# Low parts of the weights by an accumulating DMA instead of a subtraction, in a two-block fp32 transformer on one core

## The chip, the cores and the metric

The program runs on 1 core of a Trainium2 chip. The metric is device time in microseconds (us) of one execution; the kernel before takes 2588.35 us (median of 3 runs, 2588.29 to 2590.03).

Engines are named as the profile names them: PE (TensorE, matrix products), PEld (its weight loads), DVE (VectorE), ACT (ScalarE), POOL (GpSimd), SP (SyncE, which here only issues DMAs). A DMA that SP issues goes to the queue q1 (hardware_dynamic in the profile), one that POOL issues to q0 (software_dynamic). "L138" is line 138 of the kernel before.

## What is computed

512 tokens of width 1024 pass through two transformer blocks in float32. The first has a mixer (convolution branch and attention side by side), attention to a memory of 256 tokens, and a gated feed-forward with a short convolution. The second has two layers of feed-forward, mixer, feed-forward; its mixers are a pooling one and latent attention. Every part follows a normalisation and is added to the residual:

```python
h = rmsnorm(x, norm_mix_pre[l])
y = parallel_mixer(h, w_in[l], conv_dw[l], ..., w_out[l], tabs)
x = x + rmsnorm(y, norm_mix_post[l])
y = memory_cross_attention(rmsnorm(x, norm_mem_pre[l]), mem_n, w_mem_q[l], w_mem_kv[l], w_mem_o[l])
x = x + rmsnorm(y, norm_mem_post[l])
y = conv_gated_ffn(rmsnorm(x, norm_ffn_pre[l]), w_up[l], ffn_dw[l], ffn_dw_b[l], w_down[l])
x = x + rmsnorm(y, norm_ffn_post[l])
...
def swiglu(h, w_gate, w_up, w_down):
    return (jax.nn.silu(h @ w_gate) * (h @ w_up)) @ w_down
x = x + FFN_HALF * swiglu(h, ffn1_w_gate[i], ffn1_w_up[i], ffn1_w_down[i])
x = x + pool_mixer(h, pool_w[j], pool_scale[j])        # or mla_mixer(h, ...)
x = x + FFN_HALF * swiglu(rmsnorm_2(x, ffn2_norm[i]), ffn2_w_gate[i], ...)
```

Nearly all the work is in products of the 512 tokens with weights, some 225 MB of them in float32.

## The kernel before

**Products in three passes.** PE multiplies in the type float32r, which keeps fewer bits than float32. Each weight and each activation is therefore held as two parts: `hi`, the value rounded to float32r, and `lo`, what is left of it. `mm3` (L165) issues three matmuls for a product: `hi` by `hi` (L168), `hi` by the activation's `lo` (L169), and the weight's `lo` by `hi` (L170).

**Weight units.** A unit is 128 partitions of 1024 columns (512 KB; 44 or so are of 768 columns), eight 128 x 128 tiles. `load_unit` (L149) makes one: `fetch` (L127) has SP bring it into a `raw` buffer; `cook` (L132) has ACT round it into `whi` (L138), and then DVE or POOL subtract, `wlo = raw - whi` (L140). `linear` (L172) goes over output tiles, and for each over the units and their eight tiles, 24 matmuls of 512 columns per unit. There are 428 units from `load_unit`; one more, the first of all (`raw0`, L91), is cooked in four pieces. `raw`, `whi` and `wlo` have 3 buffers each, so a unit's parts can be made as soon as PE has finished with the unit three before.

**Who subtracts.** `lo_on_pool` (L144) gives a share of the units, in fourths, to POOL; the rest go to DVE. The share is set by stage: all units in the input products and the attention of the first mixer (`W_IN`, `W_KV` = 4, from L660), none for the output product, a fourth in the memory stage, none from the convolutional feed-forward on (L827).

**The other work.** In the first mixer DVE runs 24 convolution taps for each of four channel tiles (L556), six more taps run on PE with diagonal matrices that POOL builds (`dg`, L530); POOL also makes stacked parts of the queries (`st`, L426), rotary sums (`m`, L416), low parts of memory tiles (L187) and scales softmax rows (`p`, L402). In a `swiglu` stage (L867) DVE takes PSUM out (`g`, L877), ACT applies silu (L879), POOL multiplies gate by value (L882), ACT and DVE make the parts of the result (`ah` L185, `al` L187), which the second product of the stage reads. Between the stages of the first block `settle` (L349) and `pre` (L321) bring the normed result into the residual and make the new activations' parts (`xh`, `xl`, L189 and L190), with a Newton iteration on DVE (`newton`, L223) that starts from `q` (L217).

**The order of the work.** Within an engine instructions run in the order that a scheduler of the language gives them, from a simulated timeline; an instruction that waits for a semaphore holds everything behind it on its engine, or in its engine's DMA queue.

Of the kernel before, what the change touches and what calls it, by code (L numbers as in the profile page):

```python
# [26 lines left out]
# order of the taps' offsets: the even ones from the middle, then the odd ones  # L27
# [33 lines left out]
class Kern:  # L61
# [3 lines left out]
    def __init__(self, ctx, tc, a, out):  # L65
# [6 lines left out]
        self.wr = E(tc.tile_pool(name="wr", bufs=3))  # L72
        self.wh = E(tc.tile_pool(name="wh", bufs=3))
        self.wl = E(tc.tile_pool(name="wl", bufs=3))
# [3 lines left out]
        self.sp = E(tc.tile_pool(name="sp", bufs=8))  # L78
        self.yp = E(tc.tile_pool(name="yp", bufs=16))
        self.yq = E(tc.tile_pool(name="yq", bufs=3))  # L80
        self.pps = {n: E(tc.tile_pool(name=n + "_psum", bufs=b, space=bass.MemoryType.PSUM))
                    for n, b in (("ps", 2), ("sc", 2), ("pt", 2), ("po", 1), ("mi", 1))}
        self.wturn, self.wshare = 0, 0
# [19 lines left out]
    # -- small access helpers --  # L103
# [17 lines left out]
    def turn(self, out, src):  # L121
        """Transpose by PE, which moves float32 words unchanged."""
        n = src.shape[0]
        return self.nc.tensor.transpose(out, src, self.ident[:n, :n])  # L124

    # -- weights: DRAM -> raw -> exact parts hi + lo --
# [5 lines left out]
    def cook(self, raw, n, pieces=1):  # L132
        hi = self.wh.tile([P, UNIT], F32R, name="whi", tag="whi")
        lo = self.wl.tile([P, UNIT], F32R, name="wlo", tag="wlo")
        w = n // pieces
        for i in range(pieces):
            s = slice(i * w, (i + 1) * w)
            self.nc.scalar.copy(hi[:, s], raw[:, s])  # L138
            eng = self.nc.gpsimd if self.lo_on_pool() else self.nc.vector
            eng.tensor_tensor(out=lo[:, s], in0=raw[:, s], in1=hi[:, s].bitcast(F32),  # L140
                              op=ALU.subtract)
        return hi, lo

    def lo_on_pool(self):  # L144
        """Share of the units (in fourths) whose low part GpSimd makes."""
        self.wturn = (self.wturn + 1) % 4
        return self.wturn < self.wshare

    def load_unit(self, src, n=UNIT):  # L149
        return self.cook(self.fetch(src, n), n)  # L150
# [6 lines left out]
    def load_tile(self, w, nt, nk):  # L157
        """Stationary tiles of output tile nt: list over k of (hi, lo) [P, P]."""
        res = []
        for k0 in range(0, nk, 8):  # L160
            n = min(8, nk - k0)
            res += self.tiles(self.load_unit(w[nt, :, k0 * P:(k0 + n) * P], n * P), n)
        return res

    def mm3(self, ps, w, x, start, stop):  # L165
        """ps += w.T @ x with w, x each given as exact (hi, lo) parts."""
        mm = self.nc.tensor.matmul
        mm(ps, w[0], x[0], start=start, stop=False)  # L168
        mm(ps, w[0], x[1], start=False, stop=False)  # L169
        self.mmi = mm(ps, w[1], x[0], start=False, stop=stop)  # L170
# [10 lines left out]
    # -- split an fp32 tile (SBUF or PSUM), optionally scaled per partition --  # L181
# [17 lines left out]
    # -- reciprocal square roots --  # L199
    # Sums over partitions land as [32 * j + r, t]: row r of token block j; transposed, they and  # L200
    # what is made of them stand in columns, [t, j, r].
    def sums(self, pairs, nb=4, ps=None, o=0, start=True, stop=True):
        """pairs: list of (selector [P, 32], squares [P, nb * P])."""
# [9 lines left out]
    def columns(self, sm, dim, eps=0.0, w=1):  # L213
        """sm / dim + eps in columns [P, block, w], in PSUM."""
# [8 lines left out]
    def newton(self, v, n):  # L223
        """rsqrt of v [P, n] on the vector engine."""
# [14 lines left out]
    def rstd(self, sqs, dim, nb=4):  # L239
        """rsqrt(mean + eps) in columns from squares [P, nb * P], summed over the list."""  # L240
        sm = self.sums([(self.c("ones"), sq) for sq in sqs], nb)
        v = self.columns(sm, dim, EPS)
        return self.newton(v.rearrange("p j r -> p (j r)"), nb)

    @staticmethod
    def per_block(R, w):
        """The columns of the four token blocks, each repeated w times."""
        return R.unsqueeze(2).to_broadcast([P, 4, w])

    def inner_rstd(self, sm, dim, R, w=1, post=1.0):  # L250
        """post * R * rsqrt(R^2 * sm / dim + eps): the norm of rows that still lack the factor R."""
# [16 lines left out]
    def bcast_ps(self, R, nb=4, w=1):  # L268
        """Columns to rows of all partitions (row r of w in its share of them), exact float32."""
# [14 lines left out]
    def expand(self, R, w, tag="t"):  # L284
        """Columns -> [32 * block + r, tokens], zero outside the block, as exact parts."""
# [13 lines left out]
    def spread(self, X, r, tag="mi"):  # L299
        """Row r of every block, on all partitions."""  # L300
# [6 lines left out]
    # -- residual stream --  # L307
# [5 lines left out]
    def gather(self, sqs, sq, last, w=S):  # L313
        """Sum of squares so far: at most two tiles, the last one kept apart."""
# [6 lines left out]
    def pre(self, gname, dve_squares=(), tag2="xs"):  # L321
        """Gain times x as exact parts, and the reciprocal rms in quadrant form."""
# [14 lines left out]
    def post_collect(self, gname, tag="xs"):  # L337
        """Evacuation of a stage's output that a norm follows; pre() of the next stage adds it."""
# [10 lines left out]
    def settle(self):  # L349
        """Generator: adds the pending normed output to x, a tile a step."""  # L350
# [40 lines left out]
    # ------------------------------------------------------------------  # L391
    def softmax_rows(self, ps, w, f, tag):
        """softmax over ps[:, :w] * f (f: [P, 1], positive)."""
# [12 lines left out]
    def rope(self, src, g, gs, cos, sin):  # L406
        """Rotary embedding along the partitions (pairs 16 apart), gains g, gs folded in."""
# [11 lines left out]
    def stack(self, src, r, tag, on_pool=False):  # L419
        """Exact parts of the 64 rows src[64 r:], one in each half of a tile."""  # L420
# [8 lines left out]
    # -- block 1: parallel mixer --  # L429
    def mem_load(self, i):  # L430
        """Two 256-token tiles of the memory side by side."""
# [16 lines left out]
    def mem_prep(self):  # L448
        """Gain times memory as exact parts."""
# [14 lines left out]
    def mem_kv(self):  # L464
        """Generator: key and value projections of the memory, a weight unit a step."""
# [49 lines left out]
    W_IN, W_KV, W_OUT, W_MEM = 4, 4, 0, 1  # L515

    def tap(self, n):
        """Output and input ranges of tap n."""
        d = TAPS[n]
        return (slice(0, S - d), slice(d, S)) if d >= 0 else (slice(-d, S), slice(0, S + d))  # L520

    def conv_pe(self, i, at):
        """The taps of channel tile i that run on PE, as products with diagonal matrices."""
# [18 lines left out]
    def conv_taps(self, i, at, acc):  # L542
        """Generator: the other taps of channel tile i, on DVE."""
# [17 lines left out]
    def mixer(self):  # L561
# [15 lines left out]
        # n-tiles: 0..7 (gate_i, val_i), 8 k, 9 v, 10..13 q pairs  # L577
# [31 lines left out]
        def ev_k(nt, ps):  # L609
# [6 lines left out]
            # both halves of a tile hold the same kv head  # L616
# [9 lines left out]
        def ev_v(nt, ps):  # L626
# [5 lines left out]
            # [s, 64 of kv0 | 64 of kv1] per token tile; zero-padded copies per kv head  # L632
# [25 lines left out]
        for n, nt in enumerate(self.ORDER):  # L658
            if n == 2:
                self.wshare = self.W_IN  # L660
# [9 lines left out]
        self.wshare = self.W_KV  # L670
# [4 lines left out]
        # attention, one head ahead  # L675
# [46 lines left out]
        self.wshare = self.W_OUT  # L722
        # attention's part of the product first
# [13 lines left out]
    def conv_norm(self, accs, cv):  # L737
        """Generator: layernorm over the conv channels, then silu, as exact parts."""
# [17 lines left out]
        for i in range(4):  # L756
# [6 lines left out]
            # silu(n) = 0.5 * n * (1 + tanh(n / 2))  # L763
# [10 lines left out]
    # -- block 1: cross attention to the memory --  # L774
    def memory(self):
        nc = self.nc
        a = self.a
        self.wshare = self.W_MEM
# [48 lines left out]
        self.wshare = 0  # L827

    # -- block 1: conv-gated ffn --
# [36 lines left out]
    # -- block 2: swiglu --  # L866
# [28 lines left out]
    # -- block 2: pooling mixer --  # L895
    # The linear map and the pooling commute: z = rstd * (W^T (g x)) in token-major form,
    # then the window sum minus count times the token as a product with a banded matrix
    # of integers, over the count.
    def pool_mixer(self):
# [30 lines left out]
        for u, zs in enumerate(zu):  # L930
            for gg in range(2):
                g = 2 * u + gg
                B = bands[g]
                # B[0]: [first block | next | 0 | 0]; B[1]: [0 | block | next | 0]
                for n in range(2):
# [12 lines left out]
                    # the first tokens have shorter windows  # L948
# [7 lines left out]
    # -- block 2: rope tables from the positions --  # L956
# [40 lines left out]
    # -- block 2: latent attention --  # L997
# [6 lines left out]
    def mla(self):  # L1004
# [32 lines left out]
        # keys  # L1037
# [19 lines left out]
        # values: [tokens, 4 heads x 128] per chunk  # L1057
# [14 lines left out]
        # queries: per pair of heads, two nope tiles and one tile of both rope parts  # L1072
# [92 lines left out]
    def key_rstd(self, ksum, pesum, Rkv):  # L1165
        """rsqrt of the mean square of a head's key: the nope part still lacks Rkv."""
# [46 lines left out]
def _stat(w):  # L1213
    """[K, N] -> [N / 128, 128, K]: stationary tiles, each partition's data contiguous."""
# [46 lines left out]
def _axial_rope():  # L1261
    """Cosines and signed sines of the grid positions, [2, 128, tokens]."""
# [21 lines left out]
def host_arrays(i):  # L1284
# [35 lines left out]
    # w_in: (gate_i, val_i) pairs, k, v, q head pairs (i, 4 + i)  # L1320
# [9 lines left out]
    # [att | conv, u, p, (2 n-tiles, 4 k, 128)]  # L1330
# [9 lines left out]
    # [c, u, p, (kk, 512)]  # L1340
# [15 lines left out]
    # [u, p, (gg, kk, 256)]  # L1356
# [12 lines left out]
    # keys [u, p, (hh, k, 128)]; values [c, p, (k, 4 heads x 128)]  # L1369
# [23 lines left out]
```

## Time and profile before

| | us |
|---|---|
| median of 3 runs (lowest, highest) | 2588.35 (2588.29, 2590.03) |
| span of the profiled execution, first to last instruction | 2588.3 |
| PE busy | 2496.1 |
| DVE busy | 1385.5 |
| ACT busy | 919.1 |
| POOL busy | 521.8 |

No time of the profiled execution other than its span is given; the span differs from the median by 0.05 us, and the two are used as one. Matmuls are pipelined: a record of one lasts longer than the distance to the next, so the pace of PE is read as a stretch's length over its count of matmuls, and PE's idle time as the span less its busy time. "Idle before, releaser" is the time that an engine waited before an instruction, and whose end it waited for. DMA share is the part of the time in which the core's 16 DMA engines were busy, as a mean.

### The profile page before, as it was taken

The page shows a single profiled execution, that of the slowest core. Times are in us where ns is not written, and L with a number is a line of the kernel's source. Part 1 is how long each engine was busy: PE and PEld are TensorE (multiplying, and loading weights), DVE is VectorE, ACT ScalarE, POOL GpSimd, SP SyncE. Part 2 cuts the span into 40 slices and gives each one's busy share as a digit, 9 for nine tenths or more (in the row PEclk, how much of TensorE's full clock was granted, in tenths as well). Part 3 has the DMA queues.
Part 4 walks back from the last instruction along what each step waited for, and adds up shares of the span by engine and source line. Part 5 has one row for each costly group of instructions (what it writes and reads, how often), then busy time and mean ns, then how long its engine had stood idle before and what let it go on. Part 6 is the DMA issues. An engine that isn't in the chain of part 4 may idle for free.

```text
span 2588.3 us, 29365 instructions
## 1 busy us (share of the span) xinstructions
PE 2496.1 (96%) x11668; PEld 2037.2 (79%) x11668; DVE 1385.5 (54%) x1877; ACT 919.1 (36%) x1332; POOL 521.8 (20%) x417
## 2 busy tenths in 40 slices
PE   7879989899999899999999999999999999999999
PEld 6667768688888688888888888888887778888887
DVE  7997563686632645533655543555433576555522
ACT  3336534354422333322422322323222455422221
POOL 4575232311100311101211100111000144111100
PEclk9889999999999999999999999999999999999999
DMA  4211211133333222234232333223332210333232
GB/s 163 66 67 49 90 57 58 64 98 98 96 95 97 69 94 96 95 98 132 74 98 98 97 98 96 97 95 95 98 98 88 78 62 19 104 98 97 92 107 79
DMA packets 68201, 229.80 MB, mean 89 GB/s; under 512 B 7456, under 2 KB 9632, under 8 KB 68064
## 3 DMA queue, kind: packets, MB, share of 16 engines
q1 hardware_dynamic: 66688, 225.35, 27.1%
q0 software_dynamic: 1232, 2.36, 0.3%
q8 instruction: 91, 1.49, 0.2%
q14 instruction: 46, 0.38, 0.0%
q10 hardware_dynamic: 144, 0.23, 0.0%
HBM read 225.80 MB, written 2.10 MB: 88 GB/s over the span
## 4 chain that ended last, share of the span: by engine, by line
PE 86%; DVE 4%; ACT 1%; issue 0%; ACTq 0%
PE ps L169 26%; PE ps L168 26%; PE ps L170 26%; DVE x L369 1%; DVE xl L190 1%; PE wo L168 1%; PE wo L169 1%; PE wo L170 1%; PE pt L124 1%; PE po L169 0%; PE bc L274 0%; PE po L168 0%; PE po L170 0%; PE sc L168 0%; DVE wlo L140 0%
## 5 line engine op out<-in xcount | busy, mean ns | idle before, releaser
L138 ACT CAST whi<-raw 128x1024 fp32r<-128x1024 f32 (+2 forms) x432 | 440.5, 1021 | 1217.7 <-PE ps L169 767.5
L140 DVE TENSOR_TENSOR wlo<-raw,whi 128x1024 fp32r<-128x1024 f32 (+2 forms) x400 | 559.3, 1400 | 492.6 <-ACT whi L138 487.5
L169 PE MATMUL ps<-xl,whi 128*128 128x512 f32 x2008 | 789.8, 394 | 18.6 <-DVE xl L190 18.5
L168 PE MATMUL ps<-xh,whi 128*128 128x512 f32 x2008 | 784.9, 393 | 15.0 <-ACT xh L189 14.7
L170 PE MATMUL ps<-xh,wlo 128*128 128x512 f32 x2008 | 786.6, 392 | 0.0
L169 PEld LDWEIGHTS ps<-xl,whi 128*128 128x128 f32 x2008 | 380.5, 189 | 104.6 <-DVE xl L190 25.0
L168 PEld LDWEIGHTS ps<-xh,whi 128*128 128x128 f32 x2008 | 379.7, 189 | 97.3 <-ACT xh L189 16.2
L170 PEld LDWEIGHTS ps<-xh,wlo 128*128 128x128 f32 x2008 | 380.7, 190 | 79.8 <-issue 0.9
L168 PE MATMUL ps<-ah,whi 128*128 128x512 f32 x880 | 342.3, 389 | 0.0
L169 PE MATMUL ps<-al,whi 128*128 128x512 f32 x880 | 342.3, 389 | 0.0
L170 PE MATMUL ps<-ah,wlo 128*128 128x512 f32 x880 | 342.3, 389 | 0.0
L877 DVE TENSOR_TENSOR g<-ps,bct 128x512 f32<-128x512 f32 x176 | 120.6, 691 | 389.9 <-PE ps L170 382.8
L882 POOL TENSOR_TENSOR g<-g 128x512 f32<-128x512 f32 x88 | 119.0, 1353 | 856.5 <-ACT whi L138 457.6
L317 POOL TENSOR_TENSOR sq<-sq 128x512 f32<-128x512 f32 x72 | 112.7, 1566 | 535.8 <-ACT sq L310 533.9
L170 PEld LDWEIGHTS ps<-ah,wlo 128*128 128x128 f32 x880 | 165.2, 188 | 34.4
L169 PEld LDWEIGHTS ps<-al,whi 128*128 128x128 f32 x880 | 165.2, 188 | 34.2
L168 PEld LDWEIGHTS ps<-ah,whi 128*128 128x128 f32 x880 | 165.2, 188 | 34.2
L556 DVE SCALAR_TENSOR_TENSOR acc<-at,cwh,acc 128x502 f32<-128x502 f32 (+12 forms) x96 | 114.1, 1201 | 1.0 <-ACT acc L548 0.5
L140 POOL TENSOR_TENSOR wlo<-raw,whi 128x1024 fp32r<-128x1024 f32 x32 | 81.3, 2542 | 71.4 <-ACT whi L138 71.2
L185 ACT CAST ah<-g 128x512 fp32r<-128x512 f32 x88 | 54.7, 622 | 112.8 <-POOL g L882 112.8
L387 DVE SCALAR_TENSOR_TENSOR x<-ps,x 128x512 f32<-128x512 f32 x40 | 27.5, 691 | 84.5 <-PE ps L170 84.4
L858 POOL TENSOR_TENSOR c<-c 128x512 f32<-128x512 f32 x22 | 29.7, 1348 | 208.3 <-DVE c L845 178.5
(298 smaller groups left out, 2594.8 us busy)
## 6 DMA issues: line engine op xcount, KB each, us to landing
raw<-in_wgu SPq DMA_DIRECT2D x176, 512.0 KB, 3.5
raw<-in_wd SPq DMA_DIRECT2D x64, 512.0 KB, 3.5
raw<-in_w_up SPq DMA_DIRECT2D x44, 512.0 KB, 3.5
raw<-in_wd SPq DMA_DIRECT2D x32, 384.0 KB, 3.1
raw<-in_w_down SPq DMA_DIRECT2D x16, 512.0 KB, 3.5
raw<-in_w_in SPq DMA_DIRECT2D x14, 512.0 KB, 4.0
raw<-in_mla_w_in SPq DMA_DIRECT2D x9, 512.0 KB, 3.5
raw<-in_mla_w_q SPq DMA_DIRECT2D x12, 384.0 KB, 3.0
```

Of the source, the lines that this page charges most:

```text
L138: self.nc.scalar.copy(hi[:, s], raw[:, s])
L140: eng.tensor_tensor(out=lo[:, s], in0=raw[:, s], in1=hi[:, s].bitcast(F32), op=ALU.subtract)
L168: mm(ps, w[0], x[0], start=start, stop=False)
L169: mm(ps, w[0], x[1], start=False, stop=False)
L170: self.mmi = mm(ps, w[1], x[0], start=False, stop=stop)
L185: nc.scalar.copy(hi, src)
L317: self.nc.gpsimd.tensor_tensor(out=sqs[0][:, :w], in0=sqs[0][:, :w], in1=sq[:, :w], op=ALU.add)
L387: self.nc.vector.scalar_tensor_tensor(out=self.x[nt], in0=ps, scalar=scale, in1=self.x[nt], op0=ALU.mult, op1=ALU.add)
L556: nc.vector.scalar_tensor_tensor(out=acc[:, o], in0=at[:, s], scalar=w(n), in1=acc[:, o], op0=ALU.mult, op1=ALU.add)
L858: nc.gpsimd.tensor_tensor(out=c, in0=c, in1=st["g"], op=ALU.mult)
L877: nc.vector.tensor_tensor(out=g, in0=ps, in1=rb, op=ALU.mult)
L882: nc.gpsimd.tensor_tensor(out=g, in0=g, in1=st["g"], op=ALU.mult)
```

## The change

`load_unit` no longer calls `cook`. ACT writes the negated, rounded weights into the `wlo` buffer (a copy with scale -1.0, output in float32r); then a DMA that POOL issues reads the same weights from device memory a second time and adds them onto that buffer, which leaves `raw - whi`; ACT rounds `raw` into `whi` as before. `cook` stays for the first unit alone, on DVE. `lo_on_pool` and the shares are gone. `raw` has 2 buffers, `whi` and `wlo` have 4; to make room, three pools of small tiles shrink (`sp` 8 to 6, `yp` 16 to 12, `yq` 3 to 2). Comments and docstrings are dropped, so line numbers shift (L140's place is taken by 149 and 150, L138's by 151, and lines behind them move by up to 4).

```diff
-        self.wr = E(tc.tile_pool(name="wr", bufs=3))
-        self.wh = E(tc.tile_pool(name="wh", bufs=3))
-        self.wl = E(tc.tile_pool(name="wl", bufs=3))
+        self.wr = E(tc.tile_pool(name="wr", bufs=2))
+        self.wh = E(tc.tile_pool(name="wh", bufs=4))
+        self.wl = E(tc.tile_pool(name="wl", bufs=4))
...
-        self.sp = E(tc.tile_pool(name="sp", bufs=8))
-        self.yp = E(tc.tile_pool(name="yp", bufs=16))
-        self.yq = E(tc.tile_pool(name="yq", bufs=3))
+        self.sp = E(tc.tile_pool(name="sp", bufs=6))
+        self.yp = E(tc.tile_pool(name="yp", bufs=12))
+        self.yq = E(tc.tile_pool(name="yq", bufs=2))
...
             self.nc.scalar.copy(hi[:, s], raw[:, s])
-            eng = self.nc.gpsimd if self.lo_on_pool() else self.nc.vector
-            eng.tensor_tensor(out=lo[:, s], in0=raw[:, s], in1=hi[:, s].bitcast(F32),
-                              op=ALU.subtract)
+            self.nc.vector.tensor_tensor(out=lo[:, s], in0=raw[:, s],
+                                         in1=hi[:, s].bitcast(F32), op=ALU.subtract)
         return hi, lo
...
     def load_unit(self, src, n=UNIT):
-        return self.cook(self.fetch(src, n), n)
+        nc = self.nc
+        raw = self.fetch(src, n)
+        hi = self.wh.tile([P, UNIT], F32R, name="whi", tag="whi")
+        lo = self.wl.tile([P, UNIT], F32R, name="wlo", tag="wlo")
+        nc.scalar.activation(lo[:, :n], raw[:, :n], AF.Copy, scale=-1.0)
+        nc.gpsimd.dma_start(out=lo[:, :n], in_=src, accum_op=ALU.add)
+        nc.scalar.copy(hi[:, :n], raw[:, :n])
+        return hi, lo
```

On ACT in a `swiglu` stage the scheduler gave, before, one instruction per unit (`whi`) between the two that serve the stage's results (`ah`, `g`):

```order
L138 CAST whi<-raw 128x1024
L185 CAST ah<-g 128x512
L138 CAST whi<-raw 128x1024
L879 ACTIVATE g<-g 128x512
L138 CAST whi<-raw 128x1024
```

and now:

```order
L151 CAST whi<-raw 128x1024
L149 ACTIVATE wlo<-raw 128x1024
L187 CAST ah<-g 128x512
L151 CAST whi<-raw 128x1024
L149 ACTIVATE wlo<-raw 128x1024
L875 ACTIVATE g<-g 128x512
L151 CAST whi<-raw 128x1024
```

Each unit has a second ACT instruction, whose buffer is freed by the unit four before.

On POOL in the first mixer, from the second channel tile's convolution on (`vh`, `vl` are value tiles that are set to zero, `acc` a convolution sum), it stood before:

```order
L140 TENSOR_TENSOR wlo<-raw,whi 128x1024
L530 TENSOR_TENSOR dg<-con,cws 128x512
L140 TENSOR_TENSOR wlo<-raw,whi 128x1024
L638 MEMSET vh 128x4x64
L639 MEMSET vl 128x4x64
L638 MEMSET vh 128x4x64
L639 MEMSET vl 128x4x64
L140 TENSOR_TENSOR wlo<-raw,whi 128x1024
L530 TENSOR_TENSOR dg<-con,cws 128x512 x2
```

and now:

```order
L531 TENSOR_TENSOR dg<-con,cws 128x512
L150 DMA wlo<-in_w_in 128x1024 x3
L639 MEMSET vh 128x4x64
L640 MEMSET vl 128x4x64
L639 MEMSET vh 128x4x64
L640 MEMSET vl 128x4x64
L150 DMA wlo<-in_w_in 128x1024
```

The subtractions have left POOL; DMA issues stand in their places, some of them grouped, each behind a wait for ACT's negated copy.

On POOL in the latent attention, where the subtractions were DVE's before, DMA issues now stand ahead of the work on keys and softmax rows (`kraw`, `knl`, `kp` make a head's keys, `p` is a softmax row):

```order
L150 DMA wlo<-in_mla_w_q 128x768 x2
L150 DMA wlo<-in_mla_w_v 128x1024
L418 TENSOR_TENSOR m_15618<-m_15618,sh 128x512
L150 DMA wlo<-in_mla_w_out 128x1024 x3
L1095 TENSOR_TENSOR kraw<-kraw,bs 128x512
L404 TENSOR_SCALAR p<-p,rl 128x128
```

Before, this engine had no weight's instruction in that place.

## Rows read from the trace of the kernel before

**Rows 1.** The page: busy shares; the chain that ended last, by engine.

```profile
PE 2496.1 (96%) x11668; PEld 2037.2 (79%) x11668; DVE 1385.5 (54%) x1877; ACT 919.1 (36%) x1332; POOL 521.8 (20%) x417
...
PE 86%; DVE 4%; ACT 1%; issue 0%; ACTq 0%
```

**Rows 2.** Two stretches: input products with convolution; a feed-forward.

```profile
core 0: us, PE busy (x) PEld busy (x) DVE busy (x) ACT busy (x) POOL busy (x), PEclk, DMA share, GB/s
38.00:201.00 163.00, 126.76 (x633) 104.01 (x632) 160.13 (x209) 51.40 (x82) 103.77 (x64) 0.87 0.22 73
900.00:1200.00 300.00, 300.00 (x1326) 248.39 (x1325) 133.88 (x129) 88.42 (x108) 32.78 (x24) 1.00 0.31 97
```

**Rows 3.** PE's longest waits from 0 to 201 us: total, times, longest.

```profile
PE ps L168 <- DVE mk L479: 9.9, 2, 7.7
PE ps L168 <- ACT xh L189: 7.4, 1, 7.4
PE bc L274 <- DVE y L235: 6.3, 1, 6.3
PE bc L274 <- DVE f L261: 5.2, 1, 5.2
PE cps L169 <- DVE ahl L187: 4.4, 1, 4.4
```

**Rows 4.** The page's groups of the removed instructions and of ACT's rounding.

```profile
L138 ACT CAST whi<-raw 128x1024 fp32r<-128x1024 f32 (+2 forms) x432 | 440.5, 1021 | 1217.7 <-PE ps L169 767.5
L140 DVE TENSOR_TENSOR wlo<-raw,whi 128x1024 fp32r<-128x1024 f32 (+2 forms) x400 | 559.3, 1400 | 492.6 <-ACT whi L138 487.5
...
L140 POOL TENSOR_TENSOR wlo<-raw,whi 128x1024 fp32r<-128x1024 f32 x32 | 81.3, 2542 | 71.4 <-ACT whi L138 71.2
```

**Rows 5.** POOL from 38 to 201 us by line: busy, mean ns.

```profile
L140 POOL TENSOR_TENSOR wlo<-raw,whi 128x1024 fp32r<-128x1024 f32 x20 | 52.4, 2622 | 34.4 <-ACT whi L138 34.4
L530 POOL TENSOR_TENSOR dg<-con,cws 128x512 fp32r<-128x512 f32 x10 | 13.5, 1355 | 6.9 <-PE cps L170 6.8
```

**Rows 6.** DVE's convolution taps: the group from 38 to 201 us; ns min/median/max.

```profile
L556 DVE SCALAR_TENSOR_TENSOR acc<-at,cwh,acc 128x502 f32<-128x502 f32 (+12 forms) x96 | 114.1, 1201 | 1.0 <-ACT acc L548 0.5
...
L556 DVE SCALAR_TENSOR_TENSOR acc<-at,cwh,acc x96: 723/744/2904, 37.5 to 199.6; 128x504 f32<-128x504 f32 x8, 128x502 f32<-128x502 f32 x8, 128x500 f32<-128x500 f32 x8, 128x498 f32<-128x498 f32 x8
```

**Rows 7.** Timelines of DVE and POOL around 59 us: start, length.

```profile
58.38 0.74 DVE L556 SCALAR_TENSOR_TENSOR acc<-at,cwh,acc 128x505 f32<-128x505 f32 x1
59.16 2.82 DVE L556 SCALAR_TENSOR_TENSOR acc<-at,cwh,acc 128x505 f32<-128x505 f32 x1
...
59.10 2.34 POOL L140 TENSOR_TENSOR wlo<-raw,whi 128x1024 fp32r<-128x1024 f32 x1 [3.00 <-ACT whi L138]
```

**Rows 8.** The software queue: issue of band tables in ns, landing; the stretch behind.

```profile
L911 POOL DMA_DIRECT2D bd<-in_bands x4: 537/564/741, 1217.0 to 1220.4; - x4
...
DMA to landing us min/median/max: 3.2/5.0/7.0
...
1221.00:1228.00 7.00, 7.00 (x62) 5.96 (x62) 2.87 (x4) 2.20 (x3) 0.45 (x1) 1.00 1.05 344
```

**Rows 9.** The page's DMA issues: a weight unit's landing.

```profile
raw<-in_wgu SPq DMA_DIRECT2D x176, 512.0 KB, 3.5
```

**Rows 10.** The chain in order of time: first and last subtraction on it.

```profile
264.29 2.24 DVE wlo L140
...
2031.77 0.96 DVE wlo L140
```

**Rows 11.** Timelines at the start: ACT's rounding, POOL, DVE, PE's second unit.

```profile
13.62 1.03 ACT L138 CAST whi<-raw 128x1024 fp32r<-128x1024 f32 x1
...
12.81 2.48 POOL L530 TENSOR_TENSOR dg<-con,cws 128x512 fp32r<-128x512 f32 x2
...
16.43 1.21 DVE L140 TENSOR_TENSOR wlo<-raw,whi 128x1024 fp32r<-128x1024 f32 x1
...
19.75 0.39 PE L170 MATMUL ps<-xh,wlo 128*128 128x512 f32 x1
```

More of the change, by code (lines that the diff above doesn't have):

```diff
@@ L77, in __init__ @@
                                    ("tb", 4))}
-        self.sp = E(tc.tile_pool(name="sp", bufs=8))
-        self.yp = E(tc.tile_pool(name="yp", bufs=16))
-        self.yq = E(tc.tile_pool(name="yq", bufs=3))
+        self.sp = E(tc.tile_pool(name="sp", bufs=6))
+        self.yp = E(tc.tile_pool(name="yp", bufs=12))
+        self.yq = E(tc.tile_pool(name="yq", bufs=2))
         self.pps = {n: E(tc.tile_pool(name=n + "_psum", bufs=b, space=bass.MemoryType.PSUM))
                     for n, b in (("ps", 2), ("sc", 2), ("pt", 2), ("po", 1), ("mi", 1))}
-        self.wturn, self.wshare = 0, 0
         self.pending = None
@@ L138, in cook @@
             self.nc.scalar.copy(hi[:, s], raw[:, s])
-            eng = self.nc.gpsimd if self.lo_on_pool() else self.nc.vector
-            eng.tensor_tensor(out=lo[:, s], in0=raw[:, s], in1=hi[:, s].bitcast(F32),
-                              op=ALU.subtract)
+            self.nc.vector.tensor_tensor(out=lo[:, s], in0=raw[:, s],
+                                         in1=hi[:, s].bitcast(F32), op=ALU.subtract)
         return hi, lo
-    def lo_on_pool(self):
-        self.wturn = (self.wturn + 1) % 4
-        return self.wturn < self.wshare
     def load_unit(self, src, n=UNIT):
-        return self.cook(self.fetch(src, n), n)
+        nc = self.nc
[6 more added lines that the diff above has]
+        return hi, lo
     @staticmethod
@@ L514 @@
     ORDER = (0, 1, 8, 2, 3, 9, 4, 5, 10, 6, 7, 11, 12, 13)
-    W_IN, W_KV, W_OUT, W_MEM = 4, 4, 0, 1
     def tap(self, n):
@@ L659, in mixer @@
             if n == 2:
-                self.wshare = self.W_IN
                 nc.sync.dma_start(out=cos, in_=a["rope1"][0])
@@ L669, in mixer @@
         fcol = self.inner_rstd(qsum[:, :P], 64, R1, 8, post=64.0 ** -0.5)
-        self.wshare = self.W_KV
         after = self.last.ins
@@ L721, in mixer @@
                         next(cn)
-        self.wshare = self.W_OUT
         tags = ["ps", "ps", "po", "mi", "sc", "sc", "pt", "pt"]
@@ L777, in memory @@
         a = self.a
-        self.wshare = self.W_MEM
         xs, R = self.pre("g_mempre", tag2="cv")
@@ L826, in memory @@
         self.linear(a["w_mem_o"], range(8), os, evac, ("ps", "ps", "sc", "sc"))
-        self.wshare = 0
     def conv_ffn(self):
```

## The prediction

> **What bounds the kernel now.** I read the page first. PE is busy for 2496.1 of 2588.3 us and holds 86% of the chain that ended last [rows 1]; so only 92 us, the span less PE's busy time, are there to be won by keeping PE fed, plus what PE loses where its clock is granted below full. Then the stretches [rows 2]. In the feed-forward one PE never idles, at clock 1.00: 300 us over 1326 matmuls are 226 ns each, so a unit of 24 matmuls takes 5.43 us. DVE and ACT are below half there: whatever the change takes off them in such a stretch is worth nothing. From 38 to 201 us it is the other way round: DVE is busy for 160.1 of 163 us, PE for 126.8 at a mean clock of 0.87. PE's waits say the same: of the five longest before 201 us four are for DVE [rows 3]. So there are two questions: what becomes of DVE's saturated stretch, and whether the new DMA keeps a unit every 5.43 us.
>
> **What is removed.** 396 subtractions on DVE (all of L140's 400 but the first unit's four pieces) and 32 on POOL: 559.3 and 81.3 us of busy time [rows 4]. In stages where PE sets the pace this is worth nothing: DVE is at 134 of 300 us there.
>
> In the first mixer it is not DVE's but POOL's subtractions that count. POOL makes 20 of them between 38 and 201 us, 2.62 us each [rows 5], and they hold DVE up: a convolution tap that starts at 59.16, 0.06 us behind a subtraction on POOL, takes 2.82 us where the tap before took 0.74 [rows 7], and ends 0.5 us after it. Over all 96 taps the median is 0.744 us and the mean 1.201 [rows 6], an excess of 96 x 0.457 = 44 us, in a stretch where DVE is the bound. Not all of it is the subtractions': other instructions of POOL read two operands too. The subtractions are 52.4 us of POOL's work there, `dg` 13.5 [rows 5], the rest is smaller; of POOL's whole busy time in the stretch, 103.8 us [rows 2], they are half. So 0.5 x 44 = 22 us of DVE time go. Bounds: nothing at one end (the holds move to other instructions of POOL), 20 x (2.82 - 0.74) = 42 us at the other. I take 22, because it is counted from the taps themselves, and let it reach the end in full: PE's busy time leaves 163 - 127 = 36 us of room.
>
> Elsewhere subtractions stand on the chain of waits seven times, between 2.24 us (the first) and 0.96 (the last) [rows 10], some 8 us together: DVE does one ahead of the first step of a Newton iteration or of a part that PE waits for. ACT's rounding, 1.02 us, is on the chain right ahead of several of them, and a second ACT instruction now stands there. I take half, 4 us; bounds 0 and 8.
>
> **What is added, on ACT.** 428 negated copies. The nearest row is the rounding of the same shape, 1.021 us [rows 4]: 437 us, ACT at 1356 us or 52%. In the feed-forward ACT goes from 88 to some 145 of 300 us; 767.5 us of its waits before a rounding are for PE to free a buffer [rows 4], and these cover it. In the saturated stretch it is 20 more on 51.4 of 163 us. Price nothing; if the cover fails, an instruction behind a copy is late by 1.02 us.
>
> **On POOL.** 428 issues. The eight plain ones that the trace has take 0.54 to 0.74 us [rows 8]: some 240 us, and 480 if the accumulating form needs twice the time. POOL loses 81.3 and was busy for 521.8. Price nothing.
>
> **On the DMA engines.** This is the cost that no row shows. A plain unit takes 0.31 x 300 us / 55.25 units = 1.68 us of all 16 engines [rows 2] (1326 matmuls are 55.25 units). The budget is 5.43 us, so the accumulating transfer may take 3.75 us, 2.2 plain ones. Lower bound: it costs what a plain one does, and the sum is 3.36. Upper bound: two reads and a write, each as dear as a whole plain transfer, 5.04, and the sum 6.72, over the budget. I take two plain transfers, 3.36, because it moves two streams of 512 KB into the adder where a plain one moves one: sum 5.04, 93% of the budget. That is an estimate, and a tight one. What makes it looser: with a backlog on the software queue the engines reach 344 GB/s [rows 8], which is 1.52 us per 512 KB, and three times that is 4.56 us.
>
> The Trainium skill has a rule for this quantity (Collectives: The Full Stack, the section on the bandwidth ceiling): a reduction inside the DMA engine costs nothing for the addition, but needs two source reads, and ran there at 1/1.93 of a copy. By that rule the accumulating transfer would be 1.93 x 1.68 = 3.24 us, and the forecast below stands; by the upper bound from the rows it would not. No run here shows which holds.
>
> Its latency is the smaller worry. With 4 buffers a negated copy may start when PE is through with the unit four before, 3 x 5.43 = 16.3 us ahead of its use. In between lie two ACT instructions (2.1 us), a POOL multiplication that may be in front (1.3), the issue (0.6) and the landing: 3.5 us for a plain unit [rows 9], 7.0 for the worst of eight issued at once [rows 8]. 11.0 us at most: 5 us are left. SP's queue gets no longer: `raw` with 2 buffers refills when ACT has read it twice, a unit or more before it is wanted.
>
> **At the start** the second unit's low part was ready at 16.43 + 1.21 = 17.6 us, and PE wanted it at 19.75 [rows 11]. Now: ACT's copy ends near 14.7, POOL is busy with `dg` until 15.3, the issue ends at 15.9, the landing takes 3.5 to 7.0: 19.4 to 22.9. That is 0 to 3 us late; I take 1.
>
> **Sum:** 2588.35 - 22 - 4 + 1 = 2563 us. With the bounds of these terms and an accumulating transfer within its budget, 2588 - 50 = 2538 to 2588 + 3 = 2591.
>
> **Rivals.** The measurement tells about 0.2%, 5 us, from no change.
>
> *A, the forecast:* 2563, its own range 2538 to 2583. For it: DVE's saturation and the holds by POOL, both seen.
>
> *B, the accumulating queue becomes the bound; slower.* Place: every stage of plain products. It decides at 3.75 us for an accumulating transfer. At three plain transfers for it a unit takes four times 1.52 to 1.68, 6.1 to 6.7 us, where 5.43 are to be had; some 400 units lie behind the first mixer, so 2563 + 400 x 0.65 to 1.29 = 2823 to 3079. At 0.2 us over the budget it would be 2650. For it: the middle estimate leaves only 7%. Against it: the queue itself reached 344 GB/s [rows 8].
>
> The Trainium skill states (DMA: Bandwidth & Descriptors, "Issuing engines are not separate DMA queues") that transfers of all issuers share the same 16 engines and interleave, so a second queue adds no bandwidth: that is B's premise. The two queues' shares in the profile after would show it.
>
> *C, the holds move from DVE's to POOL's queue; slower.* Place: the latent attention, where POOL had no weight's work and now waits for ACT's copy ahead of keys and softmax rows. Price: POOL waited 71.4 us for 32 roundings [rows 4], 2.2 us each. The stage has 33 units; if half of the holds reach PE, 16 x 2.2 = 36 us, 2563 + 36 = 2599. It decides at 12 holds, where A's gain is gone. Against it: buffers are four deep, and the same holds stood on POOL in the mixer's attention before.
>
> *D, no change:* DVE's freed time meets another bound at once (PE's clock of 0.87, the attention's chain of scores, exponentials and transposes), and 2583 to 2593 comes out, near 2585: the 4 us of the chain and the 1 at the start alone.
>
> **How the numbers follow.** A 0.58, D 0.12, B 0.20, C 0.10. A and D together are what the traces bear out; B rests on one unknown, whose middle estimate is inside the budget but close to it; C needs many holds. So faster 0.58, same 0.12, slower 0.30. The range starts at 2535, a little below A's own, and has to take in D, C and the mild end of B to leave no more than 2 in 10 out: up to 2650.
>
> **What would show it.** Right: in the stretch that was 38 to 201 us, taps at a mean near 0.95 us and the stretch shorter by about 20; in the feed-forward still 226 ns per matmul, no wait of PE for `wlo`, a DMA share near 0.9; ACT near 1356 us, DVE at 800 to 830. B would show as PE waiting for the DMA of `wlo` in every feed-forward and a DMA share near 1; C as PE waiting in the latent attention behind POOL's `p` or `kraw`; D as taps at 0.95 us and PE's idle time unchanged. The forecast is wrong if an accumulating transfer takes over 3.75 us of the engines, or if POOL's other instructions hold DVE as long as the subtractions did.

## The result, and the profile after

The changed kernel takes 2611.24 us (2609.37 to 2614.91); the kernel before, run beside it, 2588.51. The ratio is 1.0088, 95% interval 1.0074 to 1.0102: 22.7 us **slower**, where 2563 was forecast; inside the stated range (2535 to 2650), but on the other side of the kernel before. The profiled execution of the changed kernel has a span of 2612.9 us.

The page after, to be held against [rows 1]: busy times, the two DMA queues, and the chain that ended last.

```profile
PE 2499.6 (96%) x11668; PEld 2037.1 (78%) x11668; DVE 809.7 (31%) x1481; ACT 1307.0 (50%) x1760; POOL 787.7 (30%) x813
...
q0 software_dynamic: 62864, 219.97, 47.2%
q1 hardware_dynamic: 66688, 225.35, 29.8%
...
PE 83%; DVE 7%; issue 4%; DMA 3%; ACT 2%; POOL 1%; SPq 0%; POOLq 0%; ACTq 0%; DVEq 0%
```

DVE came out where the prediction put it (800 to 830 us), ACT 49 us below its 1356. PE's busy time is 3.5 us longer, but the span less PE's busy time went from 92.2 to 113.3 us. On the chain DMA and "issue" (time in which an engine waited for nothing that the profile shows) stand with 7%, where there was nothing.

The two stretches of [rows 2], and the taps of [rows 6]:

```profile
38.00:201.00 163.00, 142.58 (x755) 114.56 (x755) 137.96 (x239) 86.31 (x131) 76.02 (x75) 0.97 0.72 168
900.00:1200.00 300.00, 300.00 (x1325) 248.53 (x1324) 52.55 (x76) 141.99 (x168) 82.28 (x83) 1.00 0.89 193
```

```profile
L557 DVE SCALAR_TENSOR_TENSOR acc<-at,cwh,acc 128x504 f32<-128x504 f32 (+12 forms) x96 | 91.4, 973 | 3.9 <-ACT acc L549 3.4
```

Both stretches went as forecast. In the mixer's first part PE gets through 755 matmuls in the 163 us, not 633, at clock 0.97, not 0.87; a tap takes 973 ns at the mean, not 1201. In the feed-forward PE still never idles, 226 ns a matmul, with the DMA engines at 0.89.

Up to the product for the convolution norm's mean, the first place of the table below, before and after:

```profile
0.00:235.60 235.60, 190.15 (x985) 153.63 (x985) 205.91 (x313) 94.11 (x159) 140.62 (x97) 0.91 0.28 95
0.00:217.20 217.20, 184.10 (x985) 145.66 (x985) 168.75 (x312) 121.46 (x190) 93.13 (x99) 0.97 0.71 173
```

DVE is busy for 37.2 us less there. The taps are 21.9 of that; most of the rest went from its other instructions, Newton steps among them. But DVE's idle time grows from 29.7 to 48.5 us, and 18.4 us arrive.

So the gain was there, and was lost behind it. This table, from the starts in PE's timeline of the product for the convolution norm's mean and of the broadcasts `bc` that end each norm, shows where (us; the changed kernel and later runs as differences from the kernel before):

```
place                         before   change  e1     e2     e5     e3     e6
conv norm's mean in mixer     235.56   -18.4   -5.0  -19.0  -18.8   -3.8  -31.1
norm behind output product    326.48    -3.2   -3.8  -20.9  -20.7   +6.3  -24.7
norm behind memory stage      465.43    +6.9   -3.9  -21.1  -17.9  +14.4  -19.0
norm ahead of latent attn.   1987.71   +12.4   -3.9  -20.4  -11.3  +18.4  -17.5
norm behind latent attn.     2243.14   +24.4   -6.2  -25.5  -15.7  +29.3  -14.2
```

Between the first two places the change gives back 15.2 us, in the memory stage 10.1, over the feed-forwards up to the fourth place and the pooling mixer 5.5, in the latent attention 12.0: 42.8 us, against 18.4 gained. From the first place to the last, before and after:

```profile
235.56:2243.14 2007.58, 1964.86 (x9177) 1601.24 (x9177) 1034.78 (x1430) 734.14 (x1066) 351.43 (x298) 0.99 0.27 87
217.17:2267.53 2050.36, 1974.26 (x9176) 1608.92 (x9177) 590.03 (x1097) 1039.48 (x1404) 613.40 (x631) 0.98 0.77 168
```

PE idles 33.4 us longer and is busy 9.4 us longer for the same matmuls. Of the latter 9.2 lie in the output product and the memory stage, where the mean granted clock is 0.94 and 0.92 instead of 1.00 and 0.98. Of the idle time 26.8 us are waits for the DMA of a low part; the longest, with one at the program's start (`in_w_in`):

```profile
PE ps L172 <- DMA wlo<-in_mla_w_out: 7.9, 1, 7.9
PE wo L172 <- DMA wlo<-in_w_out: 7.3, 2, 4.8
...
PE ps L172 <- DMA wlo<-in_w_mem_o: 5.1, 1, 5.1
PE ps L172 <- DMA wlo<-in_mla_w_in: 3.9, 1, 3.9
...
PE ps L172 <- DMA wlo<-in_w_in: 3.8, 1, 3.8
```

Each is one wait or two. The timelines of ACT, POOL and PE in the output product show one from copy to use (start, length):

```profile
282.23 1.05 ACT L149 ACTIVATE wlo<-raw 128x1024 fp32r<-128x1024 f32 x1
...
254.45 0.86 POOL L150 DMA_DIRECT2D wlo<-in_w_out  x1 [2.78 <-ACT wlo L149]
283.57 0.86 POOL L150 DMA_DIRECT2D wlo<-in_w_out  x1 [28.26 <-ACT wlo L149]
...
291.86 0.80 PE L172 MATMUL wo<-ch,wlo 128*128 128x512 f32 x1 [4.83 <-DMA wlo<-in_w_out]
```

This is the fifth of the product's eight units. The first four, issued by 254.45, hold all four buffers until PE has multiplied the last heads' results; then PE is through with them in quick succession and wants the fifth. ACT had sat between 255 and 266 us and then worked on the convolution's norm; POOL had waited 28.26 us for the copy. From the copy's start to PE's use it takes 9.6 us: 1.3 to the issue, and 8.24 from the issue to the landing.

In the output products of the memory stage and of the latent attention PE waits for the fifth of eight units too. In the latter ACT and PE show what sets the copy:

```profile
2213.38 1.05 ACT L151 CAST whi<-raw 128x1024 fp32r<-128x1024 f32 x1 [1.51 <-PE ps L171]
2214.34 1.05 ACT L149 ACTIVATE wlo<-raw 128x1024 fp32r<-128x1024 f32 x1
...
2224.99 0.79 PE L172 MATMUL ps<-oh,wlo 128*128 128x512 f32 x1 [7.88 <-DMA wlo<-in_mla_w_out]
```

ACT idles until PE frees the rounded part's buffer, rounds, and makes the copy at once; PE wants the low part at 2217.11, 2.8 us behind the copy's start, and gets it 10.7 behind. The chain of waits has eight such landings (start, length), in place of the seven subtractions of [rows 10]:

```profile
14.96 8.29 DMA wlo<-in_w_in
...
167.40 7.78 DMA wlo<-in_w_mem_v
...
283.57 8.24 DMA wlo<-in_w_out
...
435.33 8.03 DMA wlo<-in_w_mem_o
...
502.44 9.45 DMA wlo<-in_w_up
...
883.83 8.95 DMA wlo<-in_wgu
...
1996.34 8.67 DMA wlo<-in_mla_w_in
...
2215.69 9.25 DMA wlo<-in_mla_w_out
```

They are 68.7 us of the chain. Not all of it is new time, since other work stood there before; but each is a place where PE's next step hangs on a transfer, and six lie behind the mixer's gain. At these six PE wants the low part 4.8, 4.3, 9.3, 9.3, 6.1 and 2.8 us behind the copy's start, and the way takes 9.4 to 10.9. At all but the output product ACT's rounding just ahead had waited 1.4 to 4.0 us for PE to free a buffer.

Behind the wait in the output product PE's clock was first at the lower of its two levels, a granted 0.50; over 292 to 300 us, at a mean of 0.75, 27 matmuls are 296 ns each instead of 226.

```profile
291.86:295.98 4.12, 4.12 (x10) 3.25 (x11) 0.00 (x0) 0.57 (x1) 0.00 (x0) 0.50 1.04 255
292.00:300.00 8.00, 8.00 (x27) 6.45 (x28) 0.69 (x1) 2.53 (x3) 0.86 (x1) 0.75 0.89 196
```

### The profile page after: what moved, and what is told of

The parts are those of the page before. It is cut to its first block, busy times and chain, and to the rows that moved or that the text cites. A ratio compares the mean times of both kernels' runs of the same rounds, so it can differ in the third digit from the quotient of the medians.

```text
span 2612.9 us, 30445 instructions
## 1 busy us (share of the span) xinstructions
PE 2499.6 (96%) x11668; PEld 2037.1 (78%) x11668; DVE 809.7 (31%) x1481; ACT 1307.0 (50%) x1760; POOL 787.7 (30%) x813
## 3 DMA queue, kind: packets, MB, share of 16 engines
q0 software_dynamic: 62864, 219.97, 47.2%
## 4 chain that ended last, share of the span: by engine, by line
PE 83%; DVE 7%; issue 4%; DMA 3%; ACT 2%; POOL 1%; SPq 0%; POOLq 0%; ACTq 0%; DVEq 0%
PE ps L170 26%; PE ps L172 26%; PE ps L171 26%; DVE acc L557 2%; DVE x L371 1%; DVE xl L192 1%; PE pt L123 1%; ACT p L402 0%; PE bc L276 0%; PE po L171 0%; PE po L172 0%; DMA wlo<-in_w_up 0%; PE po L170 0%; DMA wlo<-in_mla_w_out 0%; POOL sq L319 0%
## 5 line engine op out<-in xcount | busy, mean ns | idle before, releaser
L151 ACT CAST whi<-raw 128x1024 fp32r<-128x1024 f32 (+1 forms) x428 | 438.9, 1026 | 965.7 <-PE ps L171 714.1
L149 ACT ACTIVATE wlo<-raw 128x1024 fp32r<-128x1024 f32 (+1 forms) x428 | 439.5, 1027 | 37.1 <-DMA raw<-in_w_in 8.7
L150 POOL DMA_DIRECT2D wlo<-in_wgu x176 | 152.8, 870 | 441.9 <-ACT wlo L149 422.9
L150 POOL DMA_DIRECT2D wlo<-in_wd x96 | 83.4, 868 | 344.9 <-ACT wlo L149 334.9
L319 POOL TENSOR_TENSOR sq<-sq 128x512 f32<-128x512 f32 x72 | 101.8, 1414 | 65.0 <-ACT sq L312 61.1
L189 DVE TENSOR_TENSOR al<-g,ah 128x512 fp32r<-128x512 f32 x88 | 61.3, 699 | 177.6 <-ACT ah L187 177.6
L557 DVE SCALAR_TENSOR_TENSOR acc<-at,cwh,acc 128x504 f32<-128x504 f32 (+12 forms) x96 | 91.4, 973 | 3.9 <-ACT acc L549 3.4
```

The costliest lines, as they stand in the source:

```text
L149: nc.scalar.activation(lo[:, :n], raw[:, :n], AF.Copy, scale=-1.0)
L150: nc.gpsimd.dma_start(out=lo[:, :n], in_=src, accum_op=ALU.add)
L151: nc.scalar.copy(hi[:, :n], raw[:, :n])
L189: self.loi = eng.tensor_tensor(out=lo, in0=src, in1=hi.bitcast(F32), op=ALU.subtract)
L319: self.nc.gpsimd.tensor_tensor(out=sqs[0][:, :w], in0=sqs[0][:, :w], in1=sq[:, :w], op=ALU.add)
L557: nc.vector.scalar_tensor_tensor(out=acc[:, o], in0=at[:, s], scalar=w(n), in1=acc[:, o], op0=ALU.mult, op1=ALU.add)
```

## The experiments

Theory 1: the steady products carry the accumulating DMA, but where a stage's units start late, the longer way to a low part is exposed (1a: by the addition; 1b: by the way as such). Theory 2: the buffers. Theory 3: the mixer's gain is worth nothing in any case. Theory 4: each transfer costs a little everywhere. The first four kernels, and three later ones, are the changed kernel with a switch per stage:

```diff
     def load_unit(self, src, n=UNIT):
         nc = self.nc
+        how = self.HOW[self.stage]
+        if how in "PVM":
+            raw = self.fetch(src, n)
...
+            eng = nc.gpsimd if how == "P" or how == "M" and self.wturn < 1 else nc.vector
+            eng.tensor_tensor(out=lo[:, :n], in0=raw[:, :n], in1=hi[:, :n].bitcast(F32),
+                              op=ALU.subtract)
+            return hi, lo
```

P subtracts on POOL, V on DVE, M on POOL for every fourth unit and on DVE for the rest; D is the accumulating DMA. `w_in0` is the program's second unit, `w_in` the other input products, `kv` the memory's keys and values.

**e1_pools**, the subtractions as before, so only the buffers differ:

```diff
+    HOW = {'w_in0': 'V', 'w_in': 'P', 'kv': 'P', 'w_out': 'V', 'mem': 'M', 'conv': 'V', 'ffn': 'V', 'pool': 'V', 'mla': 'V'}
```

> The kernel before with nothing changed but the buffers: raw 2, whi 4, wlo 4, and the three smaller pools of small tiles. Theory 1 (the loss is the longer way to a low part): the buffers matter little, 2583 to 2593 us. Theory 2 (the loss is the buffers: two raw buffers make the weights late, smaller pools hold the norms): 2600 us or more, most of the 23 us that the change lost, with PE waiting in the output product and at stage starts.

2584.68 us, ratio 0.9983 (0.9974 to 0.9992). Theory 2 falls: the buffers are worth some 4 us, of the other sign.

**e2_dma_mixer**: against e1:

```diff
-    HOW = {'w_in0': 'V', 'w_in': 'P', 'kv': 'P', 'w_out': 'V', 'mem': 'M', 'conv': 'V', 'ffn': 'V', 'pool': 'V', 'mla': 'V'}
+    HOW = {'w_in0': 'D', 'w_in': 'D', 'kv': 'D', 'w_out': 'V', 'mem': 'M', 'conv': 'V', 'ffn': 'V', 'pool': 'V', 'mla': 'V'}
```

> Accumulating DMA only for the units that the first mixer's input products and its memory keys and values use; subtractions as before everywhere else; buffers as in the change. Theory 1: the mixer keeps its gain, since in the output product and the first settle the low parts come fast again: 2565 to 2573 us, and 'mean' of the convolution's norm near 217 us as in the change. Theory 3 (the gain in the mixer is worth nothing in any case, since something later - the clock, the scheduler's order, the settle - takes it back): 2583 to 2593 us.

2567.07 us, ratio 0.9913 (0.9899 to 0.9926): faster than both kernels. The gain of 19 us at the mean's product stays to the end (table). Theory 3 falls. In the output product of this kernel the way that took 9.6 us takes 2.3, from the rounding's start to the subtraction's end:

```profile
274.97 1.03 ACT L152 CAST whi<-raw 128x1024 fp32r<-128x1024 f32 x1
...
276.03 1.23 DVE L155 TENSOR_TENSOR wlo<-raw,whi 128x1024 fp32r<-128x1024 f32 x1 [0.90 <-ACT whi L152]
```

**e3_dma_rest**, the inverse:

```diff
+    HOW = {'w_in0': 'V', 'w_in': 'P', 'kv': 'P', 'w_out': 'D', 'mem': 'D', 'conv': 'D', 'ffn': 'D', 'pool': 'D', 'mla': 'D'}
```

> The inverse: POOL and DVE subtract in the first mixer's input products and memory keys and values as before, the accumulating DMA makes every other low part. Theory 1: no gain in the mixer, all the losses behind it: 2613 to 2633 us. Theory 3: the losses belong to the mixer's end, 2588 to 2605 us.

2622.20 us, ratio 1.0131 (1.0116 to 1.0147): the losses without the gain.

**e5_dma_steady**:

```diff
+    HOW = {'w_in0': 'D', 'w_in': 'D', 'kv': 'D', 'w_out': 'V', 'mem': 'M', 'conv': 'D', 'ffn': 'D', 'pool': 'V', 'mla': 'V'}
```

> Accumulating DMA in the mixer's input products, its keys and values and in all feed-forwards (381 or so of 428 units); subtractions in the output product, the memory stage, the pooling mixer and the latent attention, the stages where units start late. Theory 1 (steady products carry the DMA, only late-started units expose it): 2565 to 2580 us. Theory 4 (each accumulating transfer costs a little everywhere, through shared DMA engines): 2595 us or more.

2574.67 us, ratio 0.9944 (0.9932 to 0.9957). 369 units have the DMA here, 340 of them in feed-forwards, and these cost 7.6 us over e2; not in the steady pace, which is 226 ns a matmul from 900 to 1200 us as before. The 36.6 us to the changed kernel lie in the output product, the memory stage, the pooling mixer and the latent attention.

**e6_plain**, the same instructions in the same order on every engine:

```diff
-        nc.gpsimd.dma_start(out=lo[:, :n], in_=src, accum_op=ALU.add)
+        nc.gpsimd.dma_start(out=lo[:, :n], in_=src)
```

> The changed kernel with the same DMA, issued by POOL at the same places, but writing instead of adding; every engine has the same instructions in the same order. The sum is left out: the low parts hold the weights themselves. Theory 1a (what is exposed is the landing of the accumulating transfer, 7.7 us): a plain one lands in 4 to 6 us and takes 1.7 us of the engines instead of 2.9, the raw units land sooner too, and some 12 exposed places give back 3 us each: 2575 to 2595 us. Theory 1b (what is exposed is the chain of ACT copy, POOL issue and queue, whatever the transfer): 2600 to 2611 us.

2576.37 us, ratio 0.9954 (0.9941 to 0.9968): 34.9 us less than the change for the word "add" alone. Theory 1a holds, but 12.7 us of it came already in the mixer (table), where nothing was expected: 4.2 us by the first norm's broadcast, 2.8 of them in PE's wait for the second unit (1.0 us instead of 3.8); the rest was not taken apart. From the mean's product on, e6 gives back 16.9 us to the last place and the change 42.8: some 26 for the addition, 17 for the way by ACT, POOL and a DMA as such. The pages' rows on queues, issues and landing (KB each, us to landing), of the changed kernel:

```profile
L150 POOL DMA_DIRECT2D wlo<-in_wgu x176 | 152.8, 870 | 441.9 <-ACT wlo L149 422.9
...
raw<-in_wgu SPq DMA_DIRECT2D x176, 512.0 KB, 6.0
wlo<-in_wgu POOLq DMA_DIRECT2D x176, 512.0 KB, 7.7
```

and of e6:

```profile
q0 software_dynamic: 62864, 219.97, 24.3%
...
L150 POOL DMA_DIRECT2D wlo<-in_wgu x176 | 98.1, 557 | 470.3 <-ACT wlo L149 456.7
...
raw<-in_wgu SPq DMA_DIRECT2D x176, 512.0 KB, 3.7
wlo<-in_wgu POOLq DMA_DIRECT2D x176, 512.0 KB, 4.8
```

The addition costs 2.9 us of landing, 2.3 more on each plain unit beside it (where [rows 9] had 3.5), and 0.3 of issue.

**e7_lead**:

```diff
-        self.wh = E(tc.tile_pool(name="wh", bufs=4))
-        self.wl = E(tc.tile_pool(name="wl", bufs=4))
+        self.wh = E(tc.tile_pool(name="wh", bufs=3))
+        self.wl = E(tc.tile_pool(name="wl", bufs=5))
```

> The changed kernel with 5 buffers for the low parts and 3 for the rounded ones instead of 4 and 4. Theory 1 (the low part is late where its buffer comes free late): a unit more of lead, 2590 to 2603 us. If instead ACT's or POOL's order sets when the copy is made, 2606 to 2616 us.

3173.20 us: far outside both. It says nothing on the low parts' lead, since the other end broke. Its chain of waits, by line:

```profile
DMA raw<-in_wgu 22%; ACT whi L151 8%; DMA raw<-in_wd 7%; DMA raw<-in_w_up 5%; ACT wlo L149 3%; PE ps L170 3%; PE ps L171 3%; DMA raw<-in_w_down 3%; PE ps L172 3%; POOL wlo L150 1%; DMA raw<-in_w_mem_o 1%; POOL g L878 1%; DMA raw<-in_mla_w_out 1%; DMA raw<-in_w_mem_k 1%; DVE y L370 1%
```

A `raw` buffer is held until ACT has rounded it too, and with 3 buffers the rounding waits for PE; the next load, one of only two, then starts late.

**e12_lead3**, the other way round:

```diff
+        self.wh = E(tc.tile_pool(name="wh", bufs=5))
+        self.wl = E(tc.tile_pool(name="wl", bufs=3))
```

> The changed kernel with 3 buffers for the low parts and 5 for the rounded ones instead of 4 and 4: a unit less of lead, 10.9 us in a feed-forward against a chain of copy, issue and landing of 9.6. Theory 1: the feed-forwards just hold or lose up to half a us a unit, and every late start exposes up to 5 us more: 2640 to 2800 us. If the lead does not matter (the scheduler's order sets when copies are made): 2605 to 2620 us.

2931.53 us, worse than the upper figure. The stretch and PE's waits:

```profile
900.00:1200.00 300.00, 265.98 (x1132) 205.29 (x1132) 67.08 (x100) 122.81 (x150) 84.88 (x78) 0.96 0.70 155
```

```profile
PE ps L172 <- DMA wlo<-in_wgu: 80.4, 99, 3.9
PE ps L172 <- DMA wlo<-in_wd: 54.9, 33, 3.2
```

A feed-forward now takes 300 us for 1132 matmuls, 265 ns each, 6.36 us a unit: a lead of 10.9 us is too short there, 16.3 us is enough. Nor are the engines the limit: their share fell to 0.70.

**e8_halves**:

```diff
-        nc.scalar.activation(lo[:, :n], raw[:, :n], AF.Copy, scale=-1.0)
-        nc.gpsimd.dma_start(out=lo[:, :n], in_=src, accum_op=ALU.add)
+        m = n // 2
+        for s in (slice(0, m), slice(m, n)):
+            nc.scalar.activation(lo[:, s], raw[:, s], AF.Copy, scale=-1.0)
+            nc.gpsimd.dma_start(out=lo[:, s], in_=src[:, s], accum_op=ALU.add)
```

> The changed kernel with the negated copy and the accumulating DMA of each unit cut into two halves of 512 columns. Theory 1a: the first tiles of a unit are ready some 3 us sooner where they are waited for, 2595 to 2608 us. Rival (POOL's and ACT's instructions, now 428 more each, or half-size descriptors that use the engines worse): 2615 us or more; feed-forward stages would then show PE waiting for wlo.

2604.51 us, ratio 1.0063 (1.0051 to 1.0076): 6.7 us off the change. The wait for `in_mla_w_out` falls from 7.9 to 4.0, that for `in_w_mem_o` from 5.1 to 2.6.

**e4_dve_mixer**: against e1:

```diff
-    HOW = {'w_in0': 'V', 'w_in': 'P', 'kv': 'P', 'w_out': 'V', 'mem': 'M', 'conv': 'V', 'ffn': 'V', 'pool': 'V', 'mla': 'V'}
+    HOW = {'w_in0': 'V', 'w_in': 'V', 'kv': 'V', 'w_out': 'V', 'mem': 'M', 'conv': 'V', 'ffn': 'V', 'pool': 'V', 'mla': 'V'}
```

> No accumulating DMA anywhere; the buffers as in the change; the subtractions of the first mixer that were POOL's are DVE's. It asks where the mixer's gain comes from. If POOL's subtractions cost DVE's taps more than the subtraction itself (the forecast's 1.1 us for each of the 20 in the stretch): DVE gets 20 to 32 subtractions of 1.4 us and loses the holds, 2588 to 2600 us against 2585 of e1_pools. If the holds are far more than that, under 2580 us; if there are none, 2605 us or more.

2574.71 us, ratio 0.9946 (0.9933 to 0.9958), 10 us faster than e1 and below the expected 2588 to 2600, with 28 more subtractions on DVE. Its taps, and e1 and this kernel up to the mean's product:

```profile
L569 DVE SCALAR_TENSOR_TENSOR acc<-at,cwh,acc 128x504 f32<-128x504 f32 (+11 forms) x96 | 87.0, 921 | 0.2
...
0.00:230.50 230.50, 187.46 (x986) 151.76 (x987) 202.92 (x314) 94.90 (x162) 143.54 (x99) 0.92 0.30 97
0.00:220.65 220.65, 182.10 (x986) 146.49 (x987) 200.65 (x342) 95.77 (x162) 78.23 (x71) 0.94 0.31 101
```

The taps are 23.5 us less than e1's 110.5. DVE's busy time is nearly the same, 202.9 and 200.7 us: what POOL's subtractions held DVE up by, at the taps and elsewhere, weighs about as much as the 28 subtractions that came. The 10 us are DVE's idle time, 20.0 instead of 27.6; why that fell is not shown. The holds are what the Trainium skill describes (SBUF — State Buffer, "Who interferes with whom"): a VectorE instruction with two SBUF inputs contends with a GpSimd instruction that reads SBUF. The runs agree: a tap takes 1.164 us at the mean in e1, 0.921 here.

**e9_gather**:

```diff
-        self.nc.gpsimd.tensor_tensor(out=sqs[0][:, :w], in0=sqs[0][:, :w], in1=sq[:, :w],
+        self.nc.vector.tensor_tensor(out=sqs[0][:, :w], in0=sqs[0][:, :w], in1=sq[:, :w],
```

> The changed kernel with the sums of squares added on DVE instead of POOL, so that POOL's queue holds no addition between two DMA issues. Rival C (a hold in POOL's queue is what makes the issues late): 2590 to 2602 us. Theory 1 (ACT's copy and the landing make them late, POOL is only the messenger): 2604 to 2614 us.

2612.02 us (2611.24 to 2615.86), as the change: additions in POOL's queue between two issues are not what makes them late.

**e11_wout**: against e2, the output product's eight units by DMA:

```diff
-    HOW = {'w_in0': 'D', 'w_in': 'D', 'kv': 'D', 'w_out': 'V', 'mem': 'M', 'conv': 'V', 'ffn': 'V', 'pool': 'V', 'mla': 'V'}
+    HOW = {'w_in0': 'D', 'w_in': 'D', 'kv': 'D', 'w_out': 'D', 'mem': 'M', 'conv': 'V', 'ffn': 'V', 'pool': 'V', 'mla': 'V'}
```

> As e2_dma_mixer, and the eight units of the mixer's output product by the accumulating DMA too. Theory 1 (their buffers come free when the last head is through, and the way to the low part is then 9.5 us instead of 2.3): 8 to 17 us worse than e2_dma_mixer, 2575 to 2584 us, with PE waiting for wlo and a lower clock behind it. If the loss at this place comes from the memory stage's units or from the settle instead: 2565 to 2571 us.

2581.40 us, ratio 0.9971 (0.9960 to 0.9983): eight units cost 14.3 us over e2. Some 7.3 are a longer busy time of PE from the mean's product to the norm (92.5 instead of 85.2 us for 422 matmuls, at a granted 0.96 and then 0.89 instead of 1.00), 6.4 are two waits:

```profile
PE wo L184 <- DMA wlo<-in_w_out: 6.4, 2, 4.1
```

**e10_first**: against e2:

```diff
-    HOW = {'w_in0': 'D', 'w_in': 'D', 'kv': 'D', 'w_out': 'V', 'mem': 'M', 'conv': 'V', 'ffn': 'V', 'pool': 'V', 'mla': 'V'}
+    HOW = {'w_in0': 'V', 'w_in': 'D', 'kv': 'D', 'w_out': 'V', 'mem': 'M', 'conv': 'V', 'ffn': 'V', 'pool': 'V', 'mla': 'V'}
```

> As e2_dma_mixer (accumulating DMA in the first mixer's input products and memory keys and values alone, 2567 us), but the second unit of the program, which PE waited 4.4 us for, is subtracted on DVE as before. Theory 1: the wait goes, the rest stays: 2561 to 2566 us. If DVE's or POOL's work at the start takes its place: 2566 to 2570 us.

2566.51 us (2563.79 to 2567.76), not told from e2's 2567.07. The wait did go, from 4.4 to 0.7 us, and at the broadcast that e2 starts at 123.51 us this kernel is 12.5 us ahead; at the mean's product it is 4.4 ahead, at the last norm 1.8. A wait that goes ahead of a bound elsewhere is worth little.

## Why the prediction was wrong

- **Holds by POOL, -22: the place was right, the size in part luck.** Over 96 taps 0.228 us each went, 21.9 us of DVE time, as worked out. But other instructions of DVE had been held too, 37.2 us went in all, and "full reach" was wrong: about half of it became idle time of DVE, and 18.4 us arrive at the mean's product. To the end of the program 17.6 come through (e2 less e1); the other 4 us of e2's gain are the buffers'.
- **Subtractions on the chain, -4: the sign was wrong.** Half of their length was counted as saved. But a low part that stands on the chain is one that is made late, and something still has to make it: after, eight issues with their landings of 7.8 to 9.5 us stand on the chain, where before it was seven subtractions of 0.5 to 2.2.
- **"Its latency is the smaller worry": the step that failed.** The 11.0 us for the way were about right (9.4 to 10.9 at the six places). The lead of 16.3 was worked out for the feed-forward and holds there (e12 shows how narrowly: 10.9 is not enough), because PE takes 5.43 us over each of the three units between. Where several units are held until an input is ready (at a stage's start, or in an output product behind attention) and then finished almost together, PE wants the next low part 2.8 to 9.3 us behind the start of its copy. This was costed at the program's start alone, not at the output product, the memory stage and the latent attention, where 37 of the 43 us were lost, in part through the lower clock behind the waits.
- **The start, +1: too small.** PE waits 3.8 us for the second unit: its low part lands at 23.25 us (14.96 and 8.29 later), behind the 22.9 that was reckoned as the latest.
- **The transfer, 3.36 us: near.** 47.2% of 2612.9 us over 419.6 units of 512 KB are 2.94 us; the plain units took 1.81, the sum 4.75 against 5.04. Beside e6, 24.3% of 2574.4, 1.49 a unit, the addition costs 1.97 times the plain transfer on the same queue. The Trainium skill's rule (Collectives: The Full Stack, the section on the bandwidth ceiling), two source reads and 1/1.93 of a copy's rate, agrees.
- **ACT and POOL at nothing: right in the steady products**; e9 moved POOL's additions and nothing changed. Rival B did not happen (0.89, no wait of PE in the stretch; its 2650 for 0.2 us over the budget should read 2643), nor C: of PE's 12.4 us more idle time in the latent attention 11.8 are waits for two low parts. D named a gain that meets another bound: for half of DVE's time it did, the rest e2 keeps. What happened was no rival of mine: a fast instruction replaced by a long transfer where the lead is short.

Settled: the mixer's gain, the place of the losses, and the addition's share in them (e2, e3, e5, e6, e11). At five of the six late places ACT's row shows the wait for PE to free a buffer; no run shows what one more buffer would give, since that broke other things (e7). Open: whether the scheduler's order on ACT adds to it at the output product, most of e6's extra gain in the mixer, and DVE's shorter idle time in e4.

## What to carry over

Moving work from a busy engine to a DMA is free only where the data are ready a transfer's landing ahead, not merely where the DMA engines have bandwidth: check the first unit behind a group that is held for a late input, not the steady pace. Choose it by stage: here 29 of 428 units hold the whole gain (e2), and eight others lose four fifths of it (e11). And before a DMA is used to take load off GpSimd, try the plain move to VectorE: it gave more than half of the gain here (e4).

## What was not expected of the hardware

- The accumulating transfer made its neighbours slower: a plain unit landed in 6.0 us beside it and in 3.7 beside a plain one, at 193 and 195 GB/s in the same stretch. POOL's issue takes 870 ns against 557.
- Here a wait cost more than its length: behind one of 4.83 us PE ran for 4.1 us at a granted 0.50, some 1.9 us lost (an estimate: 27 matmuls from 292 to 300 us, 0.07 us each). In e11 PE's longer busy time at the lower clock (7.3 us) is more than its two waits for low parts (6.4).
